# A gathered tile's end emitted amid the next tile's rows of u, and weights set between zeros eight tokens at a time

## The chip, the cores and the metric

The kernel runs on one core of a Trainium2 chip, in one launch. The metric is the device time in microseconds (us). Three runs of the kernel before gave 4913.27, 4919.69 and 4922.88 us; the median is 4919.69 us.

## The reference, cut to what matters

The reference is one decoder block on 1024 tokens of 1024 numbers. The change lies in its last part, the retrieval of experts (PEER). For every token 128 of 16384 experts are chosen (8 heads, 16 each), and

```python
act = gelu(einsum('thkd,td->thk', expert_u[eidx], tb))   # 128 dot products with rows of u
wts = g * act
y   = einsum('thk,thkd->td', wts, expert_v[eidx])            # weighted sum of 128 rows of v
x   = layer_norm(ALPHA * x + gate2 * y, ln2_g, ln2_b)
```

Here tb are the tokens, eidx the chosen experts and g the weights of the choice; the index letters are written out for reading.

## The kernel before

The tokens stand in eight tiles of 128 (a token is a partition). Tiles 1, 2 and 3 are *dense*: `dense` (line 1305) multiplies them with all 16384 experts in 128 steps on TensorE (`ps_u`, then `ps_v`), with the weights split on the chip into a high and a low part (`whi` on ScalarE line 219, `wlo` on VectorE line 220) after a load `wraw` on the queue of SyncE (SP), three buffers deep. Tiles 0, 4, 5, 6 and 7 are *gathered* (`gathered`, line 1121):

- u phase: 128 times, GpSimd (POOL) gathers one row of u for each of 128 tokens into a buffer `grow` (line 1188; 4 buffers for tile 0, 10 for the others), and VectorE multiplies it with the tile's tokens `gh2` and sums (line 1130).
- v phase: 128 times, GpSimd gathers rows of v, and TensorE multiplies a row with a narrow matrix that is zero but for one column of weights (`own`, 31 zeros on either side, so that a token's result lands on its own partition). VectorE sets that column, two tokens at a time, into one of two buffers (line 1158): 32 copies a tile. `ps_y` goes through `ys` to a scratch `y_d` in memory.
- the end, `finish` (line 1191): `gy` is loaded back, multiplied with a gate, added to the residual, normalised and stored; four rows (`gr2`: gate, residual, two parameters) are loaded for it on SP's queue. On VectorE that is five passes over a row (lines 1205, 1210, 907, 1214, 1217) and a chain of tiny instructions (lines 234 to 240).

All rows of 1024 numbers outside the gathers (`gh2`, `ys`, `gy`, `gr2`, `lnr`, the routing's `scr` and `oh`) share four buffers (`n_row`).

Generators set the order. `drive` emits a piece of the main work (the dense steps, late in the program) and then, for its cost, steps of the side work (`side`: the gathered tiles one after the other; `urgent`: the routing that picks experts for the next tiles). A scheduler with a model of times then orders the instructions of each engine; main work and the matmuls of the v phase have priority. The engines run their order strictly, each waiting at its own head. `routing` (line 1223) keeps at most two tiles picked ahead. Tile 0's phases run beside the second half of the main work, and its v phase ends when that work is over; `rows_out` (line 974) and the routing of tile 4 come after it, and the dense steps begin. Tiles 4, 5 and 6 run beside the dense steps, tile 7 alone at the end.

Of the kernel before, what the change touches and what calls it, by code (L numbers as in the profile page):

```python
# [11 lines left out]
F32 = mybir.dt.float32  # L12
# [8 lines left out]
P = 128  # L21
# [9 lines left out]
OWN = 16  # L31
# [16 lines left out]
class Block:  # L48
# [25 lines left out]
    def setup(self):  # L74
# [37 lines left out]
        )  # L112


        self.own = []
        for i in range(2):
            self.own.append(cp.tile([P, 4, 31 + OWN], F32, name=f"own{i}"))
            nc.gpsimd.memset(self.own[i], 0.0)


        self.mod_d = dr.tile([24, P], F32, name="mod_d")
# [996 lines left out]
        self.routed = fe.rearrange("p a b -> p (a b)"), g.rearrange("p a b -> p (a b)")  # L1118


    def gathered(self, tile_no):
        nc, a, gp = self.nc, self.a, self.gp
        ei, ej, g = self.picked[tile_no]
        t0 = tile_no * P
        h2 = self.row("gh2")
        nc.sync.dma_start(h2, self.h2_d[t0 : t0 + P, :])
        act = gp.tile([P, NSEL], F32, name="act", tag="act", bufs=1)
        for k in range(NSEL):
            u = self.gather(a["peer_u"], ei, k)
            nc.vector.scalar_tensor_tensor(  # L1130
                u, u, 1.0, h2, op0=ALU.mult, op1=ALU.mult, accum_out=act[:, k : k + 1]
            )
            yield 1.2
        nc.scalar.activation(act, act, AF.Gelu)
        nc.vector.tensor_tensor(act, act, g, op=ALU.mult)
        yield from self.claim("side")
        ps = self.psum("ps_wT", tag="gate")
        self.inline(nc.tensor.transpose, ps[:, :P], act, self.ident)
        wt = gp.tile([P, P], F32, name="wt", tag="wt", bufs=1)
        nc.scalar.copy(wt, ps[:, :P])  # L1140
        self.claimed = False

        n = 2 * OWN
        by = self.rows_by[self.dp is not None]
        rows = deque()
        for k in range(P + by):
            if k < P:
                b, r, half = k // n, k % n // 2, k % 2
                rows.append(self.gather(a["peer_v"], ej, b * n + half * OWN + r))
            if k >= by and k % 2:  # L1150
                j = k - by
                b, r = j // n, j % n // 2
                if r == 0:
                    yield from self.claim("side")
                    ps = self.psum("ps_y", tag="gate")
                own = self.own[r // 2 % 2]
                if r % 2 == 0:
                    nc.vector.tensor_copy(  # L1158
                        own[:, :, OWN - 1].rearrange("p (h r) -> p h r", h=2),
                        wt[:, b * n : b * n + n].rearrange("p (h r) -> p h r", h=2)[:, :, r : r + 2],  # L1160
                    )
                for half in range(2):
                    v = rows.popleft()
                    left = own[:, half * 2 + r % 2, OWN - 1 - r : OWN + 31 - r]
                    for c in range(2):
                        at = 32 * (2 * c + half)
                        self.inline(
                            nc.tensor.matmul, ps[at : at + 32, :], left, v[:, c * 512 : c * 512 + 512],
                            start=r == 0, stop=r == OWN - 1, skip_group_check=True,
                        )  # L1170
                if r == OWN - 1:
                    ys = self.row("ys")[:, :512]
                    nc.scalar.copy(ys, ps)
                    self.claimed = False
                    for half in range(2):
                        for c in range(2):
                            at = 32 * (2 * c + half)
                            t = b * n + half * OWN
                            nc.scalar.dma_start(self.y_d[tile_no, t : t + OWN, c * 512 : c * 512 + 512], ys[at : at + OWN, :])
            yield 1.2  # L1180
        y = self.row("gy")
        nc.sync.dma_start(y, self.y_d[tile_no])
        self.finish(t0, y)
        del self.picked[tile_no]

    def gather(self, table, ei, k):
        r = self.row("grow")
# [262 lines left out]
    def run(self):  # L1450
# [4 lines left out]
        self.mod2, self.picked = None, {}  # L1455
        self.missing = {hb * 4 + t for hb in range(2) for t in range(self.few[hb], 4)}
        self.turn, self.dp, self.urgent = 0, None, None
        self.claimed, self.count = False, 0
        with ExitStack() as c:
            self.gp = c.enter_context(tc.tile_pool(name="gp", bufs=1))  # L1460
            with tc.high_priority(offset=self.ahead):
                self.setup()
            self.hp = c.enter_context(tc.tile_pool(name="hp", bufs=1))
            self.wp = c.enter_context(tc.tile_pool(name="wp", bufs=1))
            with tc.tile_pool(name="bp", bufs=1) as self.bp, tc.tile_pool(name="mp", bufs=1) as self.mp:
                self.drive(self.main(), self.ratio, self.lag[0])
            with tc.tile_pool(name="dp", bufs=1) as self.dp:
                self.drive(self.dense(self.h2x), self.ratio1, self.lag[1])
                while self.side or self.urgent:
                    self.step()  # L1470


class _Cat:
# [70 lines left out]
```

## Time and profile before

| what | value |
|---|---|
| median of the runs | 4919.69 us |
| the profiled execution's own time | 4916.3 us |
| its span, first to last instruction | 4914.2 us |
| mean granted TensorE clock | 0.914 |
| busy: TensorE, VectorE, ScalarE, GpSimd | 81%, 60%, 29%, 38% |
| gathers of u, on GpSimd | 640, 859.1 us busy |
| gathers of v, on GpSimd | 640, 659.1 us busy |
| VectorE's copies of weights into `own` | 160, 28.4 us busy, 587.9 us idle before them |

The shares are averages over stages with different limits, so the prediction reads them by stage. Tile 0's v phase stands at about 2421 to 2660 us of the span; the u and v phases of tiles 4, 5 and 6, with the dense steps, from there to about 4500 us; tile 7 ends the span. In the rows below a time in brackets is how long the engine sat idle before an instruction, with what ended it. `gr` and `gh` are the profile's names of `gr2` and `gh2`, `x_d`, `h_d`, `in_ln_g` and the like of `x1_d`, `h2_d`, `ln1_g` or `ln2_g`.

### The profile page before, as it was taken

The numbers are of one execution on the slowest core, as the hardware profiler recorded it, in microseconds if no ns is written. First come the engines' busy times: TensorE is split into PE (matmuls) and PEld (weight loads), VectorE is DVE, ScalarE is ACT, GpSimd is POOL, SyncE is SP. The second block draws the span as 40 slices with busy tenths as digits, with TensorE's granted clock in tenths as the row PEclk, the third lists the DMA queues.
The fourth block names the chain that finished last, engine by engine and source line by source line (L and its number), as shares of the span: only waits on it lengthen the run. The fifth ranks groups of instructions, "written<-read, shape, count | busy, mean of one in ns | idle before, by whom it ended". The sixth has DMA issues, their size and how long they took to land.

```text
span 4914.2 us, 52631 instructions
## 1 busy us (share of the span) xinstructions
PE 3988.6 (81%) x17996; PEld 2749.0 (56%) x17996; DVE 2972.2 (60%) x6965; ACT 1414.7 (29%) x2338; POOL 1879.1 (38%) x1704
## 2 busy tenths in 40 slices
PE   6999898998999979888764777998789977896046
PEld 4667676776667757667500655556655565553000
DVE  7564645558876886976402997227962299423840
ACT  3544444323453444523100221222222222121000
POOL 1000000000145144335453366445754456544775
PEclk9999998998999989989897988999899988998579
DMA  7323233443244545655787699888988889987998
GB/s 271 108 71 116 77 105 98 147 139 112 69 121 149 169 125 176 193 165 161 221 295 263 262 335 352 300 311 323 380 320 317 311 340 337 333 290 265 380 378 352
DMA packets 441343, 1135.18 MB, mean 231 GB/s; under 512 B 141596, under 2 KB 162228, under 8 KB 441076
## 3 DMA queue, kind: packets, MB, share of 16 engines
q0 software_dynamic: 188704, 677.46, 38.1%
q1 hardware_dynamic: 126644, 405.04, 24.1%
q10 hardware_dynamic: 125728, 49.32, 3.8%
q8 instruction: 143, 2.34, 0.2%
q14 instruction: 124, 1.02, 0.1%
HBM read 1067.56 MB, written 64.11 MB: 230 GB/s over the span
## 4 chain that ended last, share of the span: by engine, by line
PE 27%; DVE 14%; DMA 9%; issue 7%; POOL 3%; ACT 1%; ACTq 0%; POOLq 0%; SPq 0%; DVEq 0%
PE ps_u L269 7%; PE ps_v L1340 7%; PE ps_y L1300 7%; DVE grow L1130 6%; DMA grow<-in_peer_v,ej 5%; DMA grow<-in_peer_u,ei 4%; POOL grow L1188 3%; DVE wlo L220 2%; PE ps_pq L269 1%; PE ps_b L269 1%; PE ps_o L269 1%; PE ps_g L269 1%; PE ps_gate L1300 1%; PE ps_z L269 1%; PE ps_x L269 0%
## 5 line engine op out<-in xcount | busy, mean ns | idle before, releaser
L1188 POOL DMA_INDIRECT grow<-in_peer_u,ei x640 | 859.1, 1342 | 734.9 <-DVE ei L1233 199.7
L1188 POOL DMA_INDIRECT grow<-in_peer_v,ej x640 | 659.1, 1030 | 628.5 <-PE ps_y L1300 503.1
L1130 DVE SCALAR_TENSOR_TENSOR grow<-grow,gh 128x1024 f32<-128x1024 f32 x640 | 765.4, 1217 | 172.8 <-DMA grow<-in_peer_u,ei 170.2
L219 ACT CAST whi<-wraw 128x1024 fp32r<-128x1024 f32 x498 | 518.5, 1047 | 994.7 <-PE ps_u L269 339.3
L220 DVE TENSOR_TENSOR wlo<-wraw,whi 128x1024 fp32r<-128x1024 f32 x498 | 606.0, 1220 | 317.9 <-ACT whi L219 283.2
L1300 PE MATMUL ps_y<-grow,own 128*32 128x512 f32 x2560 | 611.9, 622 | 117.2 <-DMA grow<-in_peer_v,ej 98.0
L1272 POOL TENSOR_SCALAR second_k<-iota_c,at 128x128 f32<-128x128 f32 x384 | 334.4, 878 | 669.0 <-PE ps_gate L1300 408.1
L269 PE MATMUL ps_u<-hhi,wlo 128*128 128x384 f32 x1024 | 379.0, 370 | 104.0 <-DVE wlo L220 103.9
L269 PE MATMUL ps_u<-hhi,whi 128*128 128x384 f32 x1024 | 373.9, 365 | 74.3 <-ACT act_t L1314 59.1
L1158 DVE COPY own<-wt 128x4 f32<-128x4 f32 x160 | 28.4, 179 | 587.9 <-PE ps_y L1300 583.7
L269 PE MATMUL ps_u<-hlo,whi 128*128 128x384 f32 x1024 | 365.2, 357 | 0.0
L975 POOL DMA_DIRECT2D h2s_d<-bighi x8 | 4.5, 563 | 927.2 <-ACT bighi L245 927.2
L1300 PEld LDWEIGHTS ps_y<-grow,own 128*32 128x32 f32 x2560 | 89.7, 109 | 460.9 <-DMA grow<-in_peer_v,ej 271.3
L1340 PE MATMUL ps_v<-wlo,ehi 128*128 128x512 f32 x768 | 267.9, 427 | 75.3 <-DVE wlo L220 75.3
L269 PEld LDWEIGHTS ps_u<-hhi,wlo 128*128 128x128 f32 x1024 | 208.8, 204 | 187.4 <-DVE wlo L220 132.2
L269 PEld LDWEIGHTS ps_u<-hhi,whi 128*128 128x128 f32 x1024 | 208.6, 204 | 143.0 <-ACT act_t L1314 70.6
L1340 PE MATMUL ps_v<-whi,elo 128*128 128x512 f32 x768 | 259.8, 415 | 0.0
L1340 PE MATMUL ps_v<-whi,ehi 128*128 128x512 f32 x768 | 214.0, 404 | 31.9 <-ACT whi L219 31.9
L1340 PEld LDWEIGHTS ps_v<-wlo,ehi 128*128 128x128 f32 x768 | 146.5, 201 | 165.2 <-DVE wlo L220 95.1
L269 PEld LDWEIGHTS ps_u<-hlo,whi 128*128 128x128 f32 x1024 | 207.7, 203 | 19.4 <-issue 16.8
L245 ACT CAST ehi<-act_t 128x384 fp32r<-128x384 f32 x128 | 65.7, 513 | 504.6 <-PE ps_v L1340 500.5
L1314 ACT ACTIVATE act_t<-ps_u 128x384 f32<-128x384 f32 x128 | 62.6, 489 | 499.6 <-PE ps_u L269 456.2
(339 smaller groups left out, 8141.5 us busy)
## 6 DMA issues: line engine op xcount, KB each, us to landing
wraw<-in_w_in SPq DMA_DIRECT2D x160, 512.0 KB, 3.6
wraw<-in_peer_uT SPq DMA_DIRECT2D x128, 512.0 KB, 6.7
wraw<-in_peer_v SPq DMA_DIRECT2D x128, 512.0 KB, 6.5
wada<-in_w_adaT SPq DMA_DIRECT2D x48, 512.0 KB, 5.4
g_d<-gs ACTq DMA_DIRECT2D x48, 512.0 KB, 4.5
gl<-g_d SPq DMA_DIRECT2D x48, 512.0 KB, 8.8
cr<-cum_d SPq DMA_DIRECT2D x64, 256.0 KB, 3.9
wraw<-in_w_ssd SPq DMA_DIRECT2D x32, 512.0 KB, 3.5
```

What stands on the lines that cost most here:

```text
L219: nc.scalar.copy(hi, raw)
L220: i = nc.vector.tensor_tensor(lo, raw, hi.bitcast(F32), op=ALU.subtract)
L245: nc.scalar.copy(hi, src)
L269: i = self.nc.tensor.matmul(ps, w[x][:, k, :], r[y][:, k, :], start=k + n == 0, stop=k == kk - 1 and n == 2)
L975: nc.gpsimd.dma_start(self.h2s_d[part][:, k, :], big[k][part][:, P * self.few[0] :])
L1130: nc.vector.scalar_tensor_tensor(u, u, 1.0, h2, op0=ALU.mult, op1=ALU.mult, accum_out=act[:, k : k + 1])
L1158: nc.vector.tensor_copy(own[:, :, OWN - 1].rearrange("p (h r) -> p h r", h=2), wt[:, b * n : b * n + n].rearrange("p (h r) -> p h r", h=2) ...
L1188: self.nc.gpsimd.indirect_dma_start(out=r, out_offset=None, in_=table, in_offset=bass.IndirectOffsetOnAxis(ap=ei[:, k : k + 1], axis=0),)
L1272: nc.gpsimd.tensor_scalar(second, self.iota_c, at[:, 1, k : k + 1], None, op0=ALU.is_equal)
L1300: return op(*args, **kw)
L1314: nc.scalar.activation(t, ps[:, :n], AF.Gelu)
L1340: nc.tensor.matmul(acc[2 * tt + c], prev[x][:, tt * P : tt * P + P], v[y].rearrange("p k c -> p (k c)")[:, c * 512 : c * 512 + 512], start ...
```

## The change

Two things are altered.

First, `gathered` no longer calls `finish` where its v phase ends. It notes the tile's number, and the next gathered tile calls `gathered_out` (the load of `gy` and `finish`) after emitting its 17th row of u (`k == 16`). For tile 7, with no tile behind it, the call comes after the last step.

Second, when the dense steps run, `own` holds eight tokens for each half and not two (`zeros(self.dp, 8)`): 8 copies a tile in the place of 32, each 16 columns wide and not 4. The two new buffers are zeroed by GpSimd. Tile 0, whose v phase is emitted earlier, keeps two tokens.

```diff
+    def zeros(self, pool, n):
+        own = []
+        for i in range(2):
+            own.append(pool.tile([P, 2, n, 31 + OWN], F32, name=f"own{n}_{i}"))
+            self.nc.gpsimd.memset(own[i], 0.0)
+        return own
...
             nc.vector.scalar_tensor_tensor(
                 u, u, 1.0, h2, op0=ALU.mult, op1=ALU.mult, accum_out=act[:, k : k + 1]
             )
+            if k == 16:
+                self.gathered_out()
             yield 1.2
...
+        owns = self.owns if self.dp else self.own
+        m = owns[0].shape[2]
...
-                own = self.own[r // 2 % 2]
-                if r % 2 == 0:
+                own = owns[r // m % 2]
+                if r % m == 0:
                     nc.vector.tensor_copy(
-                        own[:, :, OWN - 1].rearrange("p (h r) -> p h r", h=2),
-                        wt[:, b * n : b * n + n].rearrange("p (h r) -> p h r", h=2)[:, :, r : r + 2],
+                        own[:, :, :, OWN - 1],
+                        wt[:, b * n : b * n + n].rearrange("p (h r) -> p h r", h=2)[:, :, r : r + m],
                     )
...
-        y = self.row("gy")
-        nc.sync.dma_start(y, self.y_d[tile_no])
-        self.finish(t0, y)
+        self.ended = tile_no
         del self.picked[tile_no]
+
+    def gathered_out(self):
+        if self.ended is not None:
+            y = self.row("gy")
+            self.nc.sync.dma_start(y, self.y_d[self.ended])
+            self.finish(self.ended * P, y)
+            self.ended = None
...
             with tc.tile_pool(name="dp", bufs=1) as self.dp:
+                self.owns = self.zeros(self.dp, 8)
                 self.drive(self.dense(self.h2x), self.ratio1, self.lag[1])
                 while self.side or self.urgent:
                     self.step()
+                self.gathered_out()
```

What the scheduler makes of it is seen at three places. The first is VectorE behind the last copies of tile 0's v phase. Before, the end of tile 0 (`gy`) stands ahead of `rows_out` (`v`, `lnr`):

```order
L1158 COPY own_103<-wt 128x4
L1205 TENSOR_TENSOR gy<-gy,gr_16931 128x1024
L1210 SCALAR_TENSOR_TENSOR gy<-gr_16934,gy 128x1024
L907 BN_STATS ln2s<-gy 128x6 x2
...
L1214 SCALAR_TENSOR_TENSOR gy<-gy,ln2g,gr_16956 128x1024
L234 TENSOR_SCALAR ln2y<-ln2v 128x1
L991 TENSOR_TENSOR v<-v,lnr 128x1024 x4
```

Now `rows_out` follows the copies at once, and the routing of tile 4 (`val<-scr`) with it:

```order
L1167 COPY own_1_103<-wt 128x4
L988 TENSOR_TENSOR v<-v,lnr 128x1024 x4
L989 TENSOR_TENSOR v<-v,lnr 128x1024 x4
L1013 MAX val<-scr 128x8 x8
L995 TENSOR_TENSOR v<-v,lnr 128x1024
```

The end of tile 0 has moved to tile 4's u phase, between its 25th and 59th products. On SP's queue the same place read, before:

```order
L217 DMA wraw<-in_peer_uT 128x1024
L1182 DMA gy<-y_d 128x1024
L1200 DMA gr_16931<-mod_d 128x1024
...
L985 DMA lnr<-in_ln_g 128x1024
L985 DMA lnr<-in_ln_b 128x1024
L985 DMA lnr<-mod_d 128x1024
```

and now the loads of `rows_out` stand ahead, with the routing's `scr` behind all four of them:

```order
L214 DMA wraw<-in_peer_uT 128x1024
L982 DMA lnr<-in_ln_g 128x1024
L982 DMA lnr<-in_ln_b 128x1024
L982 DMA lnr<-mod_d 128x1024 x2
L1062 DMA scr<-sc_d 128x1024
```

The second place is VectorE where tile 4 ends and tile 5 begins, beside the dense steps. Before, the products of tile 5 (`grow,act<-grow,gh`) begin behind four of the five passes of tile 4's end:

```order
L220 TENSOR_TENSOR wlo<-wraw,whi 128x1024 x2
L1205 TENSOR_TENSOR gy<-gy,gr_23922 128x1024
L246 TENSOR_TENSOR elo<-act_t,ehi 128x384
L1210 SCALAR_TENSOR_TENSOR gy<-gr_23925,gy 128x1024
L220 TENSOR_TENSOR wlo<-wraw,whi 128x1024
L907 BN_STATS ln2s<-gy 128x6 x2
...
L1214 SCALAR_TENSOR_TENSOR gy<-gy,ln2g,gr_23947 128x1024
...
L220 TENSOR_TENSOR wlo<-wraw,whi 128x1024
L1332 TENSOR_TENSOR act_t<-act_t,gl 128x384
L238 TENSOR_TENSOR ln2t<-ln2y 128x1
L1130 SCALAR_TENSOR_TENSOR grow,act<-grow,gh_23954 128x1024
```

Now they begin with nothing of an end ahead of them, five splits of weights (`wlo`) earlier in the dense work, and the first pass of the end stands behind the 16th:

```order
L217 TENSOR_TENSOR wlo<-wraw,whi 128x1024
L1347 TENSOR_TENSOR act_t<-act_t,gl 128x384
L243 TENSOR_TENSOR elo<-act_t,ehi 128x384
L1135 SCALAR_TENSOR_TENSOR grow,act<-grow,gh_23900 128x1024 x9
L1013 MAX val<-scr 128x8 x7
L1135 SCALAR_TENSOR_TENSOR grow,act<-grow,gh_23900 128x1024
...
L1016 MAX val<-tkw 128x8
L1220 TENSOR_TENSOR gy<-gy,gr_24194 128x1024
```

From tile 5 to tile 6 it is six splits earlier in the same way. The third place is VectorE where the dense work is over and tile 7 begins. Before:

```order
L220 TENSOR_TENSOR wlo<-wraw,whi 128x1024
L1205 TENSOR_TENSOR gy<-gy,gr_31535 128x1024
L1210 SCALAR_TENSOR_TENSOR gy<-gr_31538,gy 128x1024
L907 BN_STATS ln2s<-gy 128x6 x2
...
L234 TENSOR_SCALAR ln2y<-ln2v 128x1
L1130 SCALAR_TENSOR_TENSOR grow,act<-grow,gh_31567 128x1024
```

and now, with the ends of the dense tiles (`dy`) between the products and tile 6's end behind the 87th of them:

```order
L217 TENSOR_TENSOR wlo<-wraw,whi 128x1024
L1135 SCALAR_TENSOR_TENSOR grow,act<-grow,gh_31465 128x1024 x7
L1224 TENSOR_TENSOR dy<-ps_v,gr_31475 128x512 x2
L1135 SCALAR_TENSOR_TENSOR grow,act<-grow,gh_31465 128x1024 x5
L1225 SCALAR_TENSOR_TENSOR dy<-gr_31479,dy 128x1024
```

In both kernels no product of tile 7 stands ahead of the last split of the dense work. SP's queue carries the same loads; the four of an end now stand between the loads of `wraw` that the dense steps of the next u phase need.

## Rows read from the trace of the kernel before

**Rows 1.** Busy time per engine by stretch; then granted clock, DMA share, GB/s.
```profile
2646.50:2702.30 55.80, 8.42 (x32) 1.21 (x32) 25.89 (x35) 0.59 (x1) 4.69 (x5) 0.65 0.68 231
2720.00:3000.00 280.00, 206.98 (x881) 174.95 (x879) 278.91 (x691) 67.23 (x90) 170.25 (x115) 0.90 0.84 306
3030.00:3340.00 310.00, 306.09 (x1412) 174.15 (x1412) 83.78 (x127) 64.70 (x90) 140.25 (x131) 0.99 0.87 309
3354.00:3374.80 20.80, 19.29 (x96) 17.08 (x95) 13.10 (x20) 5.83 (x8) 0.00 (x0) 1.00 0.83 288
3400.00:3590.00 190.00, 136.20 (x558) 112.67 (x558) 190.00 (x461) 42.20 (x57) 138.73 (x100) 0.88 0.98 374
3933.90:3960.70 26.80, 26.80 (x136) 24.34 (x136) 20.08 (x56) 9.75 (x14) 0.00 (x0) 1.00 0.75 255
4526.00:4726.00 200.00, 0.00 (x0) 0.00 (x0) 174.07 (x323) 0.26 (x1) 161.66 (x123) 0.50 0.94 355
4730.00:4890.00 160.00, 129.75 (x500) 18.66 (x494) 5.64 (x30) 1.76 (x3) 112.75 (x121) 1.00 1.02 406
```

**Rows 2.** VectorE in order of time behind tile 0's v phase.
```profile
2646.36 0.17 DVE L1158 COPY own<-wt 128x4 f32<-128x4 f32 x1 [7.32 <-PE ps_y L1300]
2670.65 1.22 DVE L1205 TENSOR_TENSOR gy<-gy,gr 128x1024 f32<-128x1024 f32 x1 [24.12 <-DMA gr<-x_d]
...
2682.18 4.62 DVE L992 TENSOR_TENSOR v<-v,lnr 128x1024 f32<-128x1024 f32 x4
...
2702.36 1.26 DVE L1016 MAX8 val<-scr 128x8 f32<-128x128 f32 x6 [2.19 <-DMA scr<-sc_d]
```

**Rows 3.** SP's queue, and TensorE's first matmul, at the same place.
```profile
2664.07 0.33 SPq L1182 DMA_DIRECT2D gy<-y_d  x1
...
2697.54 0.32 SPq L1065 DMA_DIRECT2D scr<-sc_d  x1
...
2704.36 0.69 PE L269 MATMUL ps_u<-hhi,whi 128*128 128x384 f32 x1 [44.20 <-ACT act_t L1314]
```

**Rows 4.** GpSimd in order of time: the 11th gather of tiles 5, 6, 7.
```profile
3376.29 1.75 POOL L1188 DMA_INDIRECT grow<-in_peer_u,ei  x1 [31.69 <-DVE ln2t L239]
...
3962.17 1.68 POOL L1188 DMA_INDIRECT grow<-in_peer_u,ei  x1 [39.13 <-DVE grow L1130]
...
4526.31 1.75 POOL L1188 DMA_INDIRECT grow<-in_peer_u,ei  x1 [20.37 <-DVE ln2t L238]
```

**Rows 5.** VectorE in order of time, tile 4 to tile 5.
```profile
3352.88 2.36 DVE L220 TENSOR_TENSOR wlo<-wraw,whi 128x1024 fp32r<-128x1024 f32 x2 [0.38 <-ACT whi L219]
...
3365.24 1.22 DVE L1205 TENSOR_TENSOR gy<-gy,gr 128x1024 f32<-128x1024 f32 x1
...
3374.79 1.22 DVE L1130 SCALAR_TENSOR_TENSOR grow<-grow,gh 128x1024 f32<-128x1024 f32 x1
```

**Rows 6.** VectorE in order of time, tile 5 to tile 6.
```profile
3932.63 1.23 DVE L220 TENSOR_TENSOR wlo<-wraw,whi 128x1024 fp32r<-128x1024 f32 x1 [0.38 <-ACT whi L219]
...
3960.69 1.20 DVE L1130 SCALAR_TENSOR_TENSOR grow<-grow,gh 128x1024 f32<-128x1024 f32 x1
```

**Rows 7.** VectorE in order of time, tile 6 to tile 7.
```profile
4491.95 1.23 DVE L220 TENSOR_TENSOR wlo<-wraw,whi 128x1024 fp32r<-128x1024 f32 x1
4517.60 1.22 DVE L1205 TENSOR_TENSOR gy<-gy,gr 128x1024 f32<-128x1024 f32 x1 [24.43 <-DMA gr<-mod_d]
...
4524.80 1.22 DVE L1130 SCALAR_TENSOR_TENSOR grow<-grow,gh 128x1024 f32<-128x1024 f32 x1 [1.71 <-DMA gh<-h_d]
```

**Rows 8.** Groups of gathers in tile 7's u and v phase: busy, mean ns.
```profile
L1188 POOL DMA_INDIRECT grow<-in_peer_u,ei x118 | 156.2, 1324 | 56.9 <-issue 30.2 <-DVE ln2t L238 20.4 <-DMA grow<-in_peer_u,ei 4.3
...
L1188 POOL DMA_INDIRECT grow<-in_peer_v,ej x121 | 113.5, 938 | 41.0 <-issue 27.7 <-PE ps_y L1300 7.5 <-DMA grow<-in_peer_v,ej 5.8
```

**Rows 9.** Waits on `own`: whole span, then tile 7's v phase.
```profile
DVE own L1158 <- PE ps_y L1300: 583.7, 128, 9.8
...
PE ps_y L1300 <- DVE own L1158: 7.8, 24, 0.6
```

More of the change, by code (lines that the diff above doesn't have):

```diff
@@ L112, in setup @@
         )
[L115 to L118, printed above, removed]
+        self.own = self.zeros(cp, 2)
         self.mod_d = dr.tile([24, P], F32, name="mod_d")
@@ L1163, in gathered @@
                     v = rows.popleft()
-                    left = own[:, half * 2 + r % 2, OWN - 1 - r : OWN + 31 - r]
+                    left = own[:, half, r % m, OWN - 1 - r : OWN + 31 - r]
                     for c in range(2):
@@ L1457, in run @@
         self.turn, self.dp, self.urgent = 0, None, None
-        self.claimed, self.count = False, 0
+        self.claimed, self.count, self.ended = False, 0, None
         with ExitStack() as c:
```

## The prediction, written before the changed kernel was run

> **What bounds the kernel now.** I read the stages first, since the shares over the whole span hide them: the busy time of each engine by stretch [rows 1]. Beside the dense steps the bound alternates. In a u phase VectorE is full (278.91 of 280 us in tile 4's, 190.00 of 190 in tile 5's) and TensorE is not (136.20 of 190). In a v phase TensorE is full (306.09 of 310) and VectorE is busy for 83.78. So a saving on VectorE counts in a u phase and is worth nothing in a v phase. Tile 7 at the end has no dense work beside it: in its u phase GpSimd is busy 161.66 of 200 us, VectorE 174.07, and TensorE does nothing.
>
> Then I looked at the four seams between a v phase and the next u phase, since the change lies there. At each one the same stretch table shows VectorE, the engine that bounds what follows, standing idle: 55.8 − 25.89 = 29.9 us behind tile 0; 20.8 − 13.10 = 7.7 us between tiles 4 and 5; 26.8 − 20.08 = 6.7 us between 5 and 6 [rows 1]. Between tiles 6 and 7 it waits 24.43 us in one piece, before `gy` [rows 7]. The order on VectorE and on SP's queue says why: the first pass of an end waits for its loads, and what is behind it in the row waits too. Behind tile 0, `gy` is 24.12 us late, and `rows_out` and the routing come only after it [rows 2].
>
> Third, GpSimd's waits. A gather waits when all ten buffers hold rows that no product has read. Before the 11th gather it waits 31.69, 39.13 and 20.37 us in tiles 5, 6 and 7 [rows 4]. Beside dense work that waiting costs nothing so long as VectorE is full afterwards. In tile 7 it lies on the path.
>
> **The change part by part.** The work on VectorE is the same but for 4 × 24 = 96 copies; the ends only move. So a gain is idle time that gets filled, and I price seam by seam.
>
> *A, behind tile 0.* The last copy ends at 2646.5, the first maximum of tile 4's routing starts at 2702.36 [rows 2] and TensorE's first dense product at 2704.36, after 44.20 us of idling [rows 3]. The change puts `rows_out` right behind the copies. If nothing else were late, all 29.9 us would go; that is the one bound, and zero the other. What is late next: the load of `scr` now stands behind four loads of `rows_out` on SP, all of them and tile 0's last `ys` share four buffers, and a buffer that holds `ys` is free only when it has been written out. That `gy` could be issued only at 2664.07 [rows 3] shows how long that writing took, and from issue to use `scr` took 2702.36 − 2697.54 = 4.8 us. The load that waits for that buffer would land near 2664.1 + 4.8 = 2669. `rows_out`'s passes up to there (the two groups of four, 4.62 us for one [rows 2], so 9.2 us) would be done at 2655.7, and VectorE would stand until 2669: 13 us of the 29.9 stay. Taken: −15, with a little off for the rest of the queue. The five passes of the end (about 6.3 us) are paid later, inside a full u phase, as they are paid now at the seam: no gain and no loss.
>
> *B and C, tiles 4 to 5 and 5 to 6.* The first product now follows the first split `wlo` of the stretch: it starts near 3354, not at 3374.79 [rows 5], and near 3934, not at 3960.69 [rows 6]. The idle 7.7 and 6.7 us are filled with products, and since VectorE is full from there on, the u phases end that much earlier. Taken: −7.7 and −6.7, which are the bounds on that side; zero is the other. What could take it away: five dense splits at one seam, six at the other move behind the start of the u phase. If TensorE then starves longer in the u phase (it already stands 190 − 136.20 = 53.8 us in 190), what was gained on VectorE is lost on TensorE, which has all of the v phase to do. TensorE is busy 19.29 of 20.8 us and 26.8 of 26.8 us at these seams [rows 1], so VectorE's idle time there is hidden for now; only the sum over both phases tells, and this is the weakest step.
>
> *D, tile 6 to 7.* The last split starts at 4491.95 and runs 1.23 us; then nothing stands before tile 7's first product but its own loads. So it can start near 4497, not at 4524.80 [rows 7]. GpSimd's 20.37 us before the 11th gather go [rows 4], and the phase behind them is bound by GpSimd: 156.2 us busy in 118 gathers of u, and 30.2 us idle between them for its own issuing [rows 8]. The bounds are −20.4 and −10 (as if half of the wait were replaced by one for `gh`, which now stands first in line with 1.71 us in the row [rows 7]). Against it: the five passes now run amid gathers. A gather takes 1.324 us beside products and 0.938 us in the v phase, where VectorE hardly works [rows 8]: 0.386 × 128 = 49 us over some 174 us of VectorE's work, 0.29 us for each; 6.3 us of passes cost 1.8. The eleventh gather still waits for one product, some 1.2 us. Taken: −20.4 + 1.8 + 1.2 = −17.
>
> Here a rule speaks against the change. The trace shows gathers 0.386 us longer when VectorE multiplies, and that is less than one product of 1.22 us [rows 7, 8]. The Trainium skill, "SBUF — State Buffer", section "SBUF: two separate sides", says that VectorE and GpSimd share a pair of ports as an exclusive lock, which a VectorE instruction with two inputs in that memory holds for its whole length against a GpSimd instruction that reads there. By it the passes would block gathers for all of 6.3 us, D would be −13 and the total some 4 us later. The trace agrees in sign and shows 0.29 us for each us, so I keep the trace's price.
>
> *E, eight tokens at a time.* VectorE waits 583.7 us before its copies in the whole span [rows 9], but these waits lie in v phases, where it has 226 us to spare of 310 [rows 1]: nothing is gained there. Only TensorE's waits for the copies count, and in tile 7's v phase, with no dense work to cover them, they are 7.8 us in 24 waits [rows 9]. Eight copies in place of 32 leave a quarter of the waits, each for a wider copy (16 columns for 4). The bounds are zero and −8. GpSimd is busy for 112.75 of 160 us there and the DMA share is 1.02 [rows 1], so the transfers are nearly the bound: taken −3. Zeroing the two new buffers lies on GpSimd once, under the idle time at the seam of tile 0 (0.59 us busy of 55.8 [rows 1]): nothing. The moved end of tile 7 stays where it was.
>
> *Sum.* −15 − 7.7 − 6.7 − 17 − 3 = −49.4. The profiled execution took 4916.3 us (its span 4914.2), 3.4 us under the median of the runs: 4916.3 − 49.4 = 4866.9 for a profile, and 4870 on the scale of the runs.
>
> **The rivals.**
>
> 1. *The dense block swallows it.* TensorE is nearly full at seams B and C, so filling VectorE's idle time there only shifts splits: B and C give nothing, A half (−7.5), E nothing, the tail stays (−17): −25, 4895. For it: 19.29 of 20.8 and 26.8 of 26.8 [rows 1]. Against it: in the u phases it is VectorE that is full.
>
> 2. *All idle time goes, and more.* If `scr` isn't held by a buffer (A −29.9), B and C as above, D −20.4, E −8, and the earlier start lets the next tile's routing, too, leave its waits (some −7, as one more seam of the size of C): −80, 4840. For it: `rows_out` has no loads of the end ahead of it any more. Against it: the late issue of `gy` [rows 3].
>
> 3. *Slower.* The end now loads on SP's queue in the middle of a u phase: `gy` and four rows for three tiles beside dense work. Its rows take buffers from the same four that `gh`, `scr` and the routing's rows use, and while the queue stands for a free one, the loads of `wraw` behind it stand too; that queue has three buffers ahead. If each of 12 such loads (four rows for each of tiles 0, 4 and 5) held the queue for what `gy` took from issue to use, 2670.65 − 2664.07 = 6.6 us [rows 2, 3], that is 79 us of standing for VectorE and TensorE, against A and D of −32 and nothing from the rest: +47, 4965. It decides from where SP stands longer than three weight steps last. For it: one queue in strict order. Against it: VectorE frees these buffers at a steady pace, and amid a u phase an end's loads can be issued long before they are used.
>
> 4. *It doesn't do what it says.* The next u phase starts no earlier because `gh` or the first gathers hold it, or the end waits as long amid the products as it does now ahead of them: 4915 to 4920. For it: `gh` is the row directly before the first product at tile 7. Against it: ten gathers stand finished there for 20 us [rows 4], and `gh` cost 1.71 us [rows 7].
>
> **How the numbers follow.** The forecast has 0.60, rival 1 has 0.15, rival 2 0.09, rival 3 0.09, rival 4 0.07. The likeliest case's own range, from its bounds (A 0 to −29.9, B and C halved, E 0 to −8, of which not all go one way), is 4850 to 4890. The range for 8 in 10 takes in rivals 1 and 2 and their surroundings, 4834 to 4904, and leaves out 3 and 4, 0.16. A measurement of this kernel can tell about 0.2%, 10 us, from no change. Faster: 0.60 + 0.15 + 0.09 = 0.84; the same: rival 4, 0.07; slower: rival 3, 0.09.
>
> **What would show it.** A: the row of VectorE behind the last copies has `rows_out` at once; the routing's first maximum comes some 15 us earlier after the last copy (40 us behind it, not 55.8), TensorE's first dense product too, and the wait that is left names `scr` or the load of `lnr`. B and C: no idle time before the first product, which comes within 5 us of the seam's first split; the u phases end as many us earlier as were idle. D: GpSimd's wait before the 11th gather of tile 7 is under 4 us, the first product stands under 6 us behind the last split, and the mean gather stays near 1.32 us. E: TensorE's waits for `own` in tile 7's v phase fall to some 2 us, while its v phase gets shorter by about 3. Wrong would be: the dense work's last split standing as far behind its first as now (then rival 1), SP's queue waiting for row buffers with VectorE waiting for `wraw` (rival 3), a wait as long as before at the first pass of a moved end with products held behind it (rival 4).

## The result, and the profile after

The changed kernel took 4865.41 us (median of 3, 4862.02 to 4870.32); the forecast was 4870. The ratio to the kernel before is 0.9893 (95% interval 0.987 to 0.9915). Five more rounds, beside other kernels, gave 0.9898 (0.9879 to 0.9917). The profiled execution was the slowest of the three, 4870.32 us with a span of 4868.6.

**Behind tile 0.** VectorE in order of time, after the change: the last copy of tile 0, `rows_out`, the first maximum of tile 4's routing.

```profile
2655.53 0.17 DVE L1167 COPY own<-wt 128x4 f32<-128x4 f32 x1 [7.97 <-PE ps_y L1315]
2655.61 4.62 DVE L988 TENSOR_TENSOR v<-v,lnr 128x1024 f32<-128x1024 f32 x4
2660.15 4.62 DVE L989 TENSOR_TENSOR v<-v,lnr 128x1024 f32<-128x1024 f32 x4
2681.58 1.65 DVE L1013 MAX8 val<-scr 128x8 f32<-128x128 f32 x8 [16.81 <-DMA scr<-sc_d]
```

The 24.12 us before `gy` [rows 2] are gone, and 16.81 us of waiting for `scr` stand in the place where 13 were forecast. The maximum comes 25.9 us behind the last copy and not 55.8. The forecast had 40: besides idle time, 16.7 us of VectorE's work that had stood between the two (25.89 us of work before [rows 1], 9.2 now) moved behind the maximum. SP's queue at the same place, and TensorE's first dense product:

```profile
2616.95 58.54 SPq L982 DMA_DIRECT2D lnr<-mod_d  x2
2675.59 0.38 SPq L1062 DMA_DIRECT2D scr<-sc_d  x1
...
2700.94 0.69 PE L266 MATMUL ps_u<-hhi,whi 128*128 128x384 f32 x1 [29.50 <-ACT act_t L1329]
```

The two loads of `lnr` read as one row of 58.54 us because the second was issued only near its end: the queue stood for a row buffer, and `scr` stood behind it. Which one, SP's own waits say (from 2670 to 4480 us of the span: total, times, longest):

```profile
SPq L982 <- DMA y_d<-ys: 57.7, 3, 56.9
```

It is the buffer of tile 0's last `ys`, which can only be made behind that tile's last `ps_y`. That one ended at 2660.2 us before and at 2671.4 after, 13.7 and 15.8 us behind the last copy, and SP went on 3.9 and 4.2 us later (2664.07 [rows 3] and 2675.59). TensorE's 44.20 us of idling [rows 3] are 29.50 now.

**The moved ends.** The view of one tile, `gy`, lists what VectorE stood idle for before its passes. First the kernel before, then after.

```profile
  DMA gr<-x_d: 44.1, 2
  DMA gr<-mod_d: 24.4, 1
```

```profile
  DMA gr<-x_d: 50.9, 1
```

Of the three waits before (tile 0's and tile 6's ends [rows 2, 7], and tile 7's) tile 7's alone is left, for which nothing was changed; its 50.9 us count from VectorE's last copy. Nothing waits at a moved end.

**Tile 7.** The last split, the first product, and GpSimd's 11th gather.

```profile
4465.84 1.23 DVE L217 TENSOR_TENSOR wlo<-wraw,whi 128x1024 fp32r<-128x1024 f32 x1 [0.45 <-ACT whi L216]
...
4479.31 1.23 DVE L1135 SCALAR_TENSOR_TENSOR grow<-grow,gh 128x1024 f32<-128x1024 f32 x1 [12.25 <-DMA grow<-in_peer_u,ei]
```

```profile
4490.10 1.90 POOL L1203 DMA_INDIRECT grow<-in_peer_u,ei  x1 [0.30 <-DMA grow<-in_peer_u,ei]
```

GpSimd's 20.37 us [rows 4] are 0.30. The first product now waits 12.25 us for its own gathered row, which before had long been there: it stands 13.5 us behind the last split, not 32.9 [rows 7].

**By stage.** The next table cuts each trace at the last `ps_y` of tiles 0, 4 and 6 and at tile 7's last product. "A" runs from the first cut to the second, "B, C" to the third, "D" to the fourth; "rest" is what follows. The kernels of groups 1, 2 and 3 ran on one chip within each group; group 0 is the two profiles shown so far.

| kernel | ends moved | group | A | B, C | D | rest |
|---|---|---|---|---|---|---|
| before | none | 0 | 683.2 | 1158.1 | 224.2 | 188.5 |
| changed | all | 0 | 659.1 | 1150.8 | 198.1 | 189.1 |
| own8_only | none | 1 | 680.8 | 1158.1 | 214.7 | 188.8 |
| end_only | all | 1 | 655.7 | 1147.9 | 196.1 | 190.3 |
| end6_only | tile 6 | 1 | 680.9 | 1157.7 | 197.8 | 190.9 |
| end0_only | tile 0 | 1 | 659.6 | 1156.6 | 218.4 | 191.1 |
| end45_only | tiles 4, 5 | 2 | 681.3 | 1166.8 | 211.5 | 204.2 |
| after_again | all | 2 | 660.7 | 1153.6 | 198.3 | 203.8 |
| k1 | all, earlier | 2 | 656.8 | 1154.6 | 195.6 | 203.0 |
| ys_grow | all | 2 | 577.1 | 1147.1 | 194.6 | 204.5 |
| ys_only | none | 3 | 678.8 | 1164.4 | 214.8 | 204.3 |

What lies ahead of the first cut is not touched by the change, and yet it ended between 2660.2 and 2675.5 us (ys_grow apart); a profile by itself can be 15 us off for that alone, so the stages are compared, and the ratios.

### The profile page after: what moved, and what is told of

Its sections match the earlier page's. It is cut to its first block, busy times and chain, and to the rows that moved or that the text cites. A ratio compares the mean times of both kernels' runs of the same rounds, so it can differ in the third digit from the quotient of the medians.

```text
span 4868.6 us, 52394 instructions
## 1 busy us (share of the span) xinstructions
PE 3988.5 (82%) x17996; PEld 2743.5 (56%) x17996; DVE 2958.6 (61%) x6869; ACT 1416.7 (29%) x2338; POOL 1867.9 (38%) x1706
## 3 DMA queue, kind: packets, MB, share of 16 engines
q14 instruction: 123, 1.01, 0.1%
## 4 chain that ended last, share of the span: by engine, by line
PE 26%; DVE 16%; DMA 9%; issue 7%; POOL 3%; ACT 0%; ACTq 0%; POOLq 0%; SPq 0%; DVEq 0%
DVE grow L1135 7%; PE ps_y L1315 7%; PE ps_u L266 7%; PE ps_v L1355 6%; DMA grow<-in_peer_v,ej 4%; DMA grow<-in_peer_u,ei 4%; POOL grow L1203 3%; DVE wlo L217 2%; PE ps_pq L266 1%; PE ps_b L266 1%; PE ps_x L266 1%; PE ps_o L266 1%; DVE oh L1099 1%; PE ps_gate L1315 1%; DVE oh L1103 1%
## 5 line engine op out<-in xcount | busy, mean ns | idle before, releaser
L1203 POOL DMA_INDIRECT grow<-in_peer_v,ej x640 | 659.6, 1031 | 627.9 <-PE ps_y L1315 501.2
L216 ACT CAST whi<-wraw 128x1024 fp32r<-128x1024 f32 x498 | 517.6, 1047 | 936.6 <-PE ps_u L266 277.7
L1287 POOL TENSOR_SCALAR second_k<-iota_c,at 128x128 f32<-128x128 f32 x384 | 323.2, 849 | 680.8 <-PE ps_gate L1315 419.0
L243 DVE TENSOR_TENSOR elo<-act_t,ehi 128x384 fp32r<-128x384 f32 x128 | 70.9, 554 | 297.7 <-ACT ehi L242 185.3
L1167 DVE COPY own<-wt 128x4 f32<-128x4 f32 (+1 forms) x64 | 11.1, 177 | 350.7 <-PE ps_y L1315 344.9
L1347 DVE TENSOR_TENSOR act_t<-act_t,gl 128x384 f32<-128x384 f32 x128 | 70.7, 553 | 249.9 <-ACT act_t L1329 249.9
```

The lines of the kernel that those rows point to most:

```text
L216: nc.scalar.copy(hi, raw)
L243: nc.vector.tensor_tensor(lo, src, hi.bitcast(F32), op=ALU.subtract)
L1203: self.nc.gpsimd.indirect_dma_start(out=r, out_offset=None, in_=table, in_offset=bass.IndirectOffsetOnAxis(ap=ei[:, k : k + 1], axis=0),)
L1287: nc.gpsimd.tensor_scalar(second, self.iota_c, at[:, 1, k : k + 1], None, op0=ALU.is_equal)
L1347: nc.vector.tensor_tensor(tv, tv, gt[:, :, f % 8, :], op=ALU.mult)
```

## The experiments

The theory: each seam's idle time on VectorE is a loss of its own (A, B, C, D), and the copies are worth next to nothing. The rivals: the copies shortened the dense part; the dense block swallows what is filled beside it.

**The moved ends without the wide copies.**

```diff
-        owns = self.owns if self.dp else self.own
+        owns = self.own
```

> Only the moved ends; own is set two tokens at a time as before. Theory (the time comes from the seams, the copies are worth 3 us): 49 - 3 = 46 us under the kernel before, ratio 0.9906. Rival (the copies, which VectorE holds at its head while TensorE is behind, made the dense part shorter; the dense part with tile 0's seam lost 31 us in the profile, A takes 20 of them, so 11 are the copies'): 25 + 20 = 45 less some, but then the other run, copies alone, must show 11 us.

Measured: ratio 0.9908 (0.9892 to 0.9923). That lies inside the interval of the whole change (0.9879 to 0.9917): as far as these runs can tell, the ends alone make the gain.

**The wide copies without the moved ends.**

```diff
         self.ended = tile_no
+        if True:
+            self.gathered_out()
```

> Only the copies of eight tokens; each end stands where it stood before. Theory: -3 us, ratio 0.9994, TensorE's waits for own in tile 7's v phase fall from 7.8 to about 2 us. Rival (copies count in the dense part): -11 to -14 us, ratio 0.9975.

Measured: 0.9996 (0.9986 to 1.0005). The -3 of the forecast is not excluded; the rival's -11 is. What became of TensorE's waits in tile 7's v phase shows where E went: waits of its queues (PEld loads the weights of a product, PE runs it), the kernel before, then after.

```profile
PEld ps_y L1300 <- DMA grow<-in_peer_v,ej: 103.6, 95, 1.5
PEld ps_y L1300 <- DVE own L1158: 32.7, 27, 1.5
PE ps_y L1300 <- DMA grow<-in_peer_v,ej: 17.9, 67, 1.3
```

```profile
PEld ps_y L1315 <- DMA grow<-in_peer_v,ej: 135.5, 119, 2.4
PE ps_y L1315 <- DMA grow<-in_peer_v,ej: 27.5, 111, 1.5
PEld ps_y L1315 <- DVE own L1167: 4.5, 4, 1.2
PE ps_y L1315 <- DVE own L1167: 1.5, 4, 0.6
```

The waits for `own` fell as forecast (7.8 us [rows 9] to 1.5 on PE, 32.7 to 4.5 on its weight loads), and the waits for gathered rows rose by about as much (103.6 to 135.5, 17.9 to 27.5). The stretch itself, busy times as in [rows 1], before and after:

```profile
4727.50:4891.80 164.30, 133.83 (x512) 19.50 (x512) 5.64 (x30) 1.76 (x3) 114.64 (x123) 0.99 1.01 401
```

```profile
4681.30:4846.20 164.90, 133.88 (x512) 18.65 (x512) 1.11 (x7) 1.76 (x3) 114.97 (x123) 0.99 1.01 400
```

164.30 and 164.90 us, the DMA share 1.01 in both: the transfers set this phase. What is left of E, -2 us by the ratio (-7 to +2), is too small for these runs.

**One end at a time.** In the next three the wide copies stay, and `gathered_out` is called at once for all tiles but those named.

```diff
         self.ended = tile_no
+        if tile_no != 6:            # end6_only
+        if tile_no != 0:            # end0_only
+        if tile_no not in (4, 5):   # end45_only
+            self.gathered_out()
```

> Copies of eight, and of the ends only tile 6's moves, amid tile 7's rows of u. Theory of the prediction: D = -17, with E -20, ratio 0.9959. By the profile of the changed kernel, where tile 7's first product stands 25.4 us earlier against the end of the dense work and its u phase is no longer than before: -25 - 3 = -28, ratio 0.9943. Rival (GpSimd is held by the five passes for all of their 6.3 us): -16.

Measured: 0.995 (0.9932 to 0.9969). In the table D falls from 214.7 to 197.8. All three numbers lie inside the interval, the rival's -16 too, and within a group D is 13 to 26 us shorter with the end moved. That tile 7's seam is worth about 20 us is shown; the price of the five passes amid the gathers is not told apart by this run's time (single gathers tell it, under D below).

> Copies of eight, and of the ends only tile 0's moves, amid tile 4's rows of u. Theory: A = -15 to -20 and E = -3: about -20 us, ratio 0.9959. Rival (the dense block swallows it: TensorE and VectorE have the same work to do up to the end of the dense steps, and what is early at tile 0's seam waits later): -3 to -8 us, ratio over 0.998.

Measured: 0.9968 (0.9958 to 0.9978). The rival asked for over 0.998 and falls. A is 659.6, 21 us under own8_only.

> Copies of eight, and of the ends only those of tiles 4 and 5 move, amid the rows of u of tiles 5 and 6. Prediction: B + C = -14.4 and E about 0 to -3: ratio 0.9967. By the profiles so far (from tile 0's last product to tile 6's last one, all ends moved is 6 to 12 us shorter than tile 0's alone): -6 to -12, ratio 0.9975 to 0.9988. Rival (the dense block swallows it): as the copies alone, 0.9996.

Measured: 0.9996 (0.9982 to 1.001). This is the rival's number: the ends of tiles 4 and 5 alone bring nothing that these runs can see, and the forecast's -14.4 is outside the interval (-9 to +5 us). The stretch B, C was 1166.8 us; with no end moved it was 1164.4 us in group 3 and 1157.7 to 1158.1 in groups 0 and 1, so it got no shorter. With the other ends moved as well it did: within group 1 from 1156.6 us (tile 0's end alone) or 1158.1 (none) to 1147.9, in group 0 from 1158.1 to 1150.8, 7 to 10 us. The ratios leave room for such a dependence but don't prove it: against the copies alone tile 0's end brings 14 us, tile 6's 23 and those of tiles 4 and 5 none, 36 together, and all ends bring 43 to 51; the gap is within their noise.

**Where B and C went.** The stretches from tile 4's last `ps_y` through seam, u phase, seam, v phase of tile 5, before and then after:

```profile
3343.40:3374.80 31.40, 27.76 (x135) 24.19 (x136) 16.47 (x23) 10.29 (x14) 0.94 (x1) 1.00 0.89 326
3374.80:3623.40 248.60, 175.85 (x723) 145.08 (x722) 248.60 (x572) 54.31 (x73) 181.38 (x127) 0.89 0.95 352
3623.40:3642.90 19.50, 19.50 (x96) 17.68 (x95) 13.24 (x22) 6.35 (x10) 2.80 (x2) 0.95 0.68 244
3642.90:3920.60 277.70, 275.37 (x1297) 152.54 (x1296) 67.76 (x104) 55.49 (x77) 132.84 (x126) 1.00 0.89 326
```

```profile
3330.60:3344.50 13.90, 13.22 (x63) 11.29 (x63) 4.69 (x6) 5.23 (x8) 0.94 (x1) 1.00 1.01 402
3344.50:3610.50 266.00, 189.41 (x801) 156.50 (x801) 264.93 (x594) 59.00 (x80) 174.64 (x124) 0.90 0.91 333
3610.50:3622.10 11.60, 9.95 (x45) 8.85 (x47) 4.90 (x7) 3.34 (x6) 5.01 (x5) 0.85 1.03 408
3622.10:3914.00 291.90, 288.65 (x1342) 160.67 (x1341) 69.14 (x86) 58.67 (x82) 133.00 (x127) 1.00 0.87 316
```

The u phase begins 13.90 us behind tile 4 and not 31.40. But it lasts 17.4 us longer: VectorE is full in it, and from tile 4's last `ps_y` to its end VectorE does 265.1 us of work before and 269.6 after, so the idle time that was filled (14.9 us before, 10.3 after) went to other work. In the v phase TensorE is busy for 275.37 of 277.7 and 288.65 of 291.9 us, with 1297 matmuls before and 1342 after; the 45 more are those that no longer stood ahead of it (954 before, 909 after). Over the four stretches it is the same 2251 matmuls, in 577.2 us before and 583.4 after: B alone brought nothing, and cost 6.2 us here.

C did otherwise. The stretches from tile 5's last `ps_y` through seam, u phase and v phase of tile 6, before and then after:

```profile
3920.60:3960.70 40.10, 35.84 (x172) 32.54 (x173) 24.22 (x60) 13.75 (x19) 1.88 (x2) 0.96 0.69 235
3960.70:4207.70 247.00, 173.84 (x714) 145.81 (x713) 246.97 (x540) 51.95 (x71) 173.78 (x126) 0.87 0.94 350
4207.70:4501.50 293.80, 288.92 (x1322) 156.55 (x1321) 71.24 (x113) 57.47 (x81) 134.58 (x128) 1.00 0.85 300
```

```profile
3914.00:3933.30 19.30, 17.17 (x78) 15.17 (x77) 8.26 (x26) 5.03 (x7) 0.94 (x1) 0.91 0.78 300
3933.30:4194.10 260.80, 194.66 (x802) 161.15 (x802) 260.80 (x574) 59.91 (x80) 196.13 (x126) 0.88 0.94 345
4194.10:4481.40 287.30, 285.54 (x1343) 161.40 (x1341) 71.91 (x93) 59.37 (x83) 129.37 (x125) 1.00 0.86 308
```

Tile 6's u phase ends 280.1 us behind tile 5's last `ps_y` and not 287.1, the 7 us of the forecast, and its v phase is 6.5 us shorter. In end45_only that u phase ends after 280.5 us too, but tile 5's stage ahead of it takes 591.1 us. What makes that stage so much longer there stays open: from the end of the u phase it has 1393 matmuls, own8_only 1389. That TensorE, full in the v phases, takes back what VectorE gains is so far argued, not shown.

If that is the cause, the gain must appear where TensorE has less to do. Two kernels leave out a third of the dense steps' second product; thin_all moves all ends, thin_06 those of tiles 0 and 6 only:

```diff
-                    for x, y in ((0, 0), (0, 1), (1, 0)):
+                    for x, y in ((0, 0), (1, 0)):
```

> The change, with a third of the dense steps' second product left out (ps_v without the low part of the weights, 4 matmuls for each pair of halves in place of 6), so that TensorE has time to spare in the v phases. To be read against the next kernel, from tile 4's last ps_y to tile 6's. Theory (what B and C gave on VectorE was lost because TensorE is full in the v phases): with that taken away, moving the ends of tiles 4 and 5 makes this stretch 8 to 14 us shorter. Rival (the seams' idle time never was a loss): no difference, under 4 us.

> As the kernel above with the same third left out, but the ends of tiles 4 and 5 stand where they stood before; only those of tiles 0 and 6 move. Theory: 8 to 14 us longer than the one above, in its time and from tile 4's last ps_y to tile 6's. Rival: the same within 4 us.

Measured: thin_all 0.9641 (0.9616 to 0.9667), 4752.35 us; thin_06 0.9677 (0.9651 to 0.9703), 4773.47 us on the same chip. From tile 4's last `ps_y` to tile 6's, thin_06 first:

```profile
3291.50:4370.80 1079.30, 875.88 (x3954) 611.95 (x3954) 685.27 (x1377) 250.63 (x343) 620.79 (x507) 0.90 0.93 349
```

```profile
3288.90:4347.90 1059.00, 862.08 (x3954) 591.33 (x3954) 682.29 (x1377) 250.20 (x343) 637.63 (x509) 0.92 0.95 356
```

With less work on TensorE the move of these two ends is worth 1079.3 - 1059.0 = 20.3 us in the stage, and 21 in the medians. The intervals of the ratios overlap a little, but no run of one kernel reaches those of the other (4746.76 to 4756.33 and 4766.37 to 4779.22 us): the rival's "under 4 us" falls; that it is more than the 8 to 14 expected is not shown, since stage D, for which the two kernels differ in nothing, is some 10 us shorter in the same pair of profiles. Two reserves. The same pair with all of TensorE's work, the ends of tiles 0 and 6 alone beside all ends, was not run; the nearest is the stage in group 1, 1156.6 against 1147.9, where it is worth 8.7 us. And TensorE is nearly full in the thin kernels' v phases too (240.97 of 244.6 us in thin_all's for tile 5). In this pair tile 5's u phase does end earlier against tile 4's last `ps_y`, 274.7 us for 282.3, and the v phase behind it gives nothing back, 252.7 for 259.2. So the runs favour that TensorE's work decides what such a move is worth; how it takes the gain back in the full kernel they don't show.

**The end earlier in the row.**

```diff
-            if k == 16:
+            if k == 1:
```

> As the change, but the end is emitted after the second row of u and not after the 17th: in VectorE's row the first pass of tile 6's end stands behind 11 products of tile 7 and not behind 87, those of tiles 4 and 5 behind 12 and 11. Theory (what costs is VectorE standing at the end's first pass until its loads land, some 25 us behind the dense work, and 11 products cover 13 us of that): the wait comes back in part, about 10 us at tile 7, with ten gathered rows ahead of it, and a few at tile 5 and 6: 10 to 15 us over the changed kernel, ratio 0.9915 to 0.993. Rival (it suffices that the product stands ahead at all; where the end stands amid the rows is the same): the ratio of the changed kernel, 0.9895.

Measured: 0.9906 (0.9889 to 0.9922) against 0.9898 (0.9879 to 0.9917) beside it: no difference that the intervals can tell, though they take in the lower end of the theory too (0.9915). The expectation failed on a number. VectorE at tile 7 in this kernel, the first product and the first pass of tile 6's end:

```profile
4472.26 1.23 DVE L1135 SCALAR_TENSOR_TENSOR grow<-grow,gh 128x1024 f32<-128x1024 f32 x1 [8.60 <-issue]
...
4495.00 1.23 DVE L1220 TENSOR_TENSOR gy<-gy,gr 128x1024 f32<-128x1024 f32 x1 [0.71 <-DMA gr<-mod_d]
```

Eleven products took 22.7 us and not 13, since their rows came in at the pace of the gathers; the wait left was 0.71 us. So this run doesn't test what a wait amid the rows costs: there was none.

> The changed kernel itself beside the others, for comparison on one chip: ratio 0.989 to 0.991, by its first runs and by the sum of the single steps (0.9950 for tile 6's end with the copies, 0.9968 for tile 0's, and 0.998 for the two between).

Measured: 0.9898 (0.9879 to 0.9917), as said above.

**What still held tile 0's seam.** SP stood for tile 0's last `ys`. One edit takes it out of the four row buffers:

```diff
-                    ys = self.row("ys")[:, :512]
+                    ys = self.row("grow" if b == P // n - 1 and not self.dp else "ys")[:, :512]
```

> As the change, but tile 0's last ys takes one of that tile's gather buffers, which nobody needs any more, and not one of the four row buffers. Theory of step A (the 16.8 us that VectorE still stands for scr is SP's queue standing for the fourth load of rows_out until that ys has been written out): scr is issued some 10 to 14 us earlier, and the dense steps begin so much earlier: 10 to 14 us under the changed kernel, ratio 0.987. Rival (something else is late at that seam, the dense work's memory or the routing's own chain): within 3 us of the changed kernel.

Measured: 0.9813 (0.9795 to 0.9831), 4842.91 us: 41 us under the changed kernel on the same chip, not 10 to 14, and faster than both kernels. VectorE, SP and TensorE:

```profile
2615.44 0.17 DVE L1167 COPY own<-wt 128x4 f32<-128x4 f32 x1 [6.52 <-PE ps_y L1315]
2615.51 4.62 DVE L988 TENSOR_TENSOR v<-v,lnr 128x1024 f32<-128x1024 f32 x4
2620.06 4.62 DVE L989 TENSOR_TENSOR v<-v,lnr 128x1024 f32<-128x1024 f32 x4
2624.60 0.16 DVE L1167 COPY own<-wt 128x4 f32<-128x4 f32 x1
```

```profile
2621.84 0.32 SPq L1062 DMA_DIRECT2D scr<-sc_d  x1
```

```profile
2656.89 0.69 PE L266 MATMUL ps_u<-hhi,whi 128*128 128x384 f32 x1 [4.56 <-ACT act_t L1329]
```

`rows_out` no longer follows the last copy: it stands between copies of tile 0, `scr` is issued 53.8 us earlier than in the changed kernel, and the dense steps begin 44 us earlier, beside the rest of tile 0's v phase. Tile 0's last `ps_y` comes at 2717.9, and the kernel is faster all the same. I had priced one load in a given order; with the buffer free, the order itself was another.

> Copies of eight and tile 0's last ys in a gather buffer, as in the kernel that was fastest so far (ratio 0.9813), but every end stands where it stood before. Theory (two things hold rows_out behind tile 0: its end at the head of VectorE's and SP's rows, and the row buffer; with the end in its old place the buffer alone frees nothing): within 5 us of the kernel before, ratio over 0.999. Rival (the buffer was the cause, and moving tile 0's end was not needed for it): the whole difference to the changed kernel, some 40 us, ratio near 0.9915.

Measured: 0.9983 (0.9971 to 0.9996). The buffer alone is worth about 8 us (2 to 14), a little more than the theory's 5, and a fifth of what it is worth with the ends moved. `gy` stands ahead again, and waits:

```profile
2671.68 1.23 DVE L1222 TENSOR_TENSOR gy<-gy,gr 128x1024 f32<-128x1024 f32 x1 [23.91 <-DMA gr<-mod_d]
```

Both things held the seam, the end at the head of the row and the buffer; each taken away alone leaves the other.

## Why the prediction was right, step by step

The total was right, 4870 forecast and 4865.41 measured. That it came so near is in part luck: B, C and E gave less than their terms, D and the dense part behind A gave more.

- A: forecast -15, measured about -14 by the ratios of end0_only and own8_only, and -21 to -25 in the stage (five kernels with tile 0's end in its place took 678.8 to 683.2 us, those with it moved 655.7 to 660.7). The mechanism was right to the wait that would be late next (`scr`, 16.81 us for 13). Its reason was right in part: the buffer came free late because tile 0's v phase ended late, and the writing of `ys` was only the last 4 us of it. VectorE from the last `ps_y` to the end of tile 4's u phase, before and after:

```profile
2660.20:3036.30 376.10, 244.66 (x1040) 209.82 (x1040) 351.19 (x875) 77.48 (x106) 197.92 (x137) 0.85 0.83 303
```

```profile
2671.40:3027.40 356.00, 241.01 (x1031) 203.70 (x1030) 340.48 (x866) 77.27 (x105) 184.59 (x138) 0.86 0.84 314
```

  The stretch is 20.1 us shorter. Counted from the last copy, as the forecast counted, VectorE's idle time fell from 38.6 us (24.9, and the 13.7 between the copy and the last `ps_y`) to 22.1 (15.5, and 15.8 less the 9.2 of `rows_out`): 16.5 us, the forecast's 15. The rest of the stage's 24.1 us in this pair is 2.1 because the last `ps_y`, the cut, came later behind the copy, 1.5 less work, and 3.9 in tile 4's v phase (307.1 to 303.2 us), for which the forecast had no term.
- B and C: forecast -14.4 together, measured nothing by end45_only (0.9996) and -7 to -10 in the stage, within a group, when the other ends move too. The step that failed is "since VectorE is full from there on, the u phases end that much earlier", and with it that the gain lasts through the next v phase. Tile 5's u phase ends no earlier against tile 4 (280.0 us from its last `ps_y` before, 279.9 after); tile 6's does, by 7.0 us, but tile 5's v phase is 6.3 us longer, from the end of the u phase (297.2 to 303.5). The first product did not follow without idle time either: of the 13.90 us at the seam VectorE worked 4.69. The prediction named this as its weakest step and priced it in rival 1; for these two seams rival 1 came nearer than the forecast when they move alone, for A and D it did not. Its sign, the last split of the dense work as far behind its first product as before, did not show: 1787.6 us before and 1764.9 after.
- D: forecast -17, measured -13 to -26 in the stage, about -20 in the mean (211.5 to 224.2 us with tile 6's end in its place, 194.6 to 198.3 with it moved) and -23 by the ratios of end6_only and own8_only. GpSimd's wait went as told. The term that was mis-sized is the 1.8 us taken off for longer gathers: 126 gathers of the changed kernel's u phase, with the five passes among them, take 1239 ns in the mean, 118 of own8_only's 1257 and of [rows 8] 1324. The forecast took a mean for a price of each us of VectorE's work; single gathers show a lock. Tile 7 of the changed kernel, in order of time, with the pass of L1229 at the end:

```profile
4622.89 1.22 DVE L1135 SCALAR_TENSOR_TENSOR grow<-grow,gh 128x1024 f32<-128x1024 f32 x1
4622.94 1.99 POOL L1203 DMA_INDIRECT grow<-in_peer_u,ei  x1 [0.30 <-issue]
...
4635.18 0.94 POOL L1203 DMA_INDIRECT grow<-in_peer_u,ei  x1 [0.30 <-DMA grow<-in_peer_u,ei]
4635.20 1.23 DVE L1135 SCALAR_TENSOR_TENSOR grow<-grow,gh 128x1024 f32<-128x1024 f32 x1
...
4636.67 1.27 DVE L1229 SCALAR_TENSOR_TENSOR gy<-gy,ln2g,gr 128x1024 f32<-128x1024 f32 x1
4637.67 1.08 POOL L1203 DMA_INDIRECT grow<-in_peer_u,ei  x1 [0.30 <-DMA grow<-in_peer_u,ei]
```

  A gather that begins just behind the start of a product ends 0.8 us behind that product's end; one that begins ahead of a product takes 0.94 us. Of this phase's 128 gathers 76 began with more than 0.13 us of a product or pass left to run, and 73 of them took what was left and 0.8 us; the other 52 took under 1.0 us. This is what the Trainium skill ("SBUF — State Buffer", "SBUF: two separate sides") calls an exclusive lock, and the trace agrees. But a gather is held only by the instruction that is under way as it begins, and of the five passes one met a gather so, with 0.27 us left: that gather took 1.08 us. So the passes cost some 0.1 us, and not the 1.8 of the sum or the 6.3 that the prediction worked out from the rule.

  What the forecast for the profile missed: the first product was to stand under 6 us behind the last split and stands 13.5 behind, held by its gathered row.
- E: forecast -3, measured nothing in the phase (v phase of tile 7 164.3 and 164.9 us) and -2 (-7 to +2) by the ratio of own8_only. The waits for `own` fell as told, and the waits for gathered rows took their place.
- Rival 2 had as its condition that no buffer holds `scr`. In the changed kernel one does; ys_grow takes it away, and the time falls by 41 us, more than the 30 that rival promised over the forecast, but by another order of the work and not by that rival's terms.
- Rival 3 (SP's queue stands for row buffers; its +47 makes 4967 on the scale of the runs, not 4965): the queue did stand, 58.54 us, but at tile 0's seam. It stood there before too, with `gy` issued only at 2664.07 [rows 3]; ys_grow shows what it still cost. Beside the dense work the loads of an end stood for a buffer three times, 7.8 us at the longest, and ScalarE's part of the split waited 2.1 us in all for `wraw`, against 5.8 before: nothing starved.
- Rival 4 (the end waits as long amid the products) asked for a wait at the first pass of a moved end; the view of `gy` above has none.

By stages the sum is -23 (A), -7 to -10 (B, C), -20 (D) and 0 (E): -50 to -53 for -49.4.

## What to carry to other kernels

An instruction that waits for loads at the head of an in-order engine costs what stands behind it, so put work that is ready ahead of it; but count the gain only where that engine is the bound through the next phase as well. At the two seams here with a full TensorE in the phase behind, 14.4 us of idle time to be filled gave nothing by themselves and 7 to 10 us beside the other ends. Where one wait goes, look at once for the buffer that holds the queue next: here all ends and the buffer together were worth 1.9%, the ends alone 1.0% (tile 0's by itself 0.3%), and the buffer alone 0.2%. Work moved past a boundary is to be priced on both sides of it. And a mean that is longer beside another engine's work is not yet a price per us: look at single instructions.

## What the runs showed of the hardware that was not expected

In tile 7 of the changed kernel a gather that GpSimd begins while VectorE is in a product ends 0.8 us behind the product's end, up to 1.99 us in all; one that begins ahead of the product takes 0.94 us (the lines under D).

From tile 7's last product to the end the span took 188.5 to 191.1 us in groups 0 and 1 and 203.0 to 204.5 us in groups 2 and 3, whatever the kernel. The difference went with the group and lies in tile 7's v phase, in which the gathers move the same rows: 164.2 us at 402 GB/s in own8_only (group 1), 179.7 us at 367 GB/s in after_again (group 2) and 180.4 us at 366 GB/s in ys_only (group 3). What makes it was not tried; the kernel before took 4908.6 us in group 1 and 4930.7 and 4932.7 in groups 2 and 3, so ratios are compared within a group only.
